# Hybrid SSD and attention block: shared inverse roots in the final norm, and the last halves weighted on the vector engine

## The chip, the cores and the metric

The kernel runs on one core of one Trainium2 chip. The metric is the device time of one execution in microseconds. Engines are named as in the profile: PE (TensorE matmul; PEld its weight loads), DVE (VectorE), ACT (ScalarE), POOL (GpSimd), SP (SyncE, which issues all transfers here).

## The reference

One layer of a hybrid decoder block on a 1024 x 1024 stream: a Mamba-2 branch and a windowed attention branch, mixed by gates, then a SwiGLU feed-forward part, then the final norm. The change lies in the last two lines: the down projection and the norm of its result.

```python
def rmsnorm(x, g):
    xf = x.astype(jnp.float32)
    y = xf * lax.rsqrt(jnp.mean(xf * xf, axis=-1, keepdims=True) + EPS)
    return (y * g.astype(jnp.float32)).astype(x.dtype)
...
        h = rmsnorm(x, norm_ffn[l])
        x = x + (jax.nn.silu(h @ w_ffn_gate[l]) * (h @ w_ffn_up[l])) @ w_ffn_down[l]
    return rmsnorm(x, norm_final)
```

## The kernel before

The stream x of 1024 tokens stands as eight row blocks of 128 tokens, numbered jj = 0 to 7; each block has two halves b = 0 and 1 of 512 columns. At the end of the kernel all of it lies in one tile xr (128 partitions, 8 blocks, 1024 columns), nfin holds norm_final on every partition, and jk takes the squares that nobody reads.

The down projection is done as seven matrix products after Strassen's and Winograd's scheme, in the order PRODUCTS = (1, 2, 3, 5, 7, 6, 4). The list INTO says to which quarters (th, b) of the output a product adds: th picks blocks 0 to 3 or 4 to 7, b the half. Each product has four row blocks j. Matrices are used as two parts, a high one (an ACT cast) and a low one (a DVE subtraction, "split" below), and every tile product takes three matmuls, so PE waits for these casts and splits. Products 6 and 4 are the last: product 6 adds to (0, 1), (1, 0) and (1, 1), which ends the work on blocks 0 to 3 and on the right halves of blocks 4 to 7; product 4 adds to (1, 0), the left halves of blocks 4 to 7. In product 4, the last four of the inner steps are run row block by row block (n_tail = 4), so block 4 is ended first and block 7 last.

down_out takes each result out of PSUM with a DVE SCALAR_TENSOR_TENSOR ("eviction" below: half of it is added to xr), and behind the final eviction of each half it starts out_half(jj, b). That function squares the half on ACT with a sum over the columns (tile osq, a slot of two sums for each block), multiplies the half by nfin on POOL in place, and, for the second half of a block, has inverse_root compute the root of that block's mean square by twelve 128x1 instructions on DVE: the sum, a shift and a subtraction on the bits for a first guess, and three Newton steps of three instructions each. Then ACT scales the right half, DVE the left half, and SP issues one transfer for each, 256 KB.

The order of instructions on each engine comes from a planner (the class Pace): it runs the kernel's tasks against estimated times, and a task issues its next instructions when the planner thinks that its inputs are there. For blocks 0 to 3 inverse_root yields to the planner behind every instruction, so that those roots are strewn between other work; for blocks 4 to 7 it does not, and a root stands in one piece. Small tiles come from the function small(tag, width), where each pair of tag and width has four slots in rotation. Every recorded instruction carries the line of the recording helper, L169, so rows are told apart by their tiles.

Of the kernel before, what the change touches and what calls it, by code (L numbers as in the profile page):

```python
# [14 lines left out]
AF = mybir.ActivationFunctionType  # L15
ALU = mybir.AluOpType
# [4 lines left out]
P = 128  # L21
S = 1024
D = 1024
# [9 lines left out]
EPS = 1e-6  # L33
# [303 lines left out]
def hybrid_block(ctx, tc, x, norm_mix, w_in, b_gate, conv_w, conv_b, dt_bias, a_log, d_skip, ssm_norm,  # L337
# [3 lines left out]
    nc = Core(tc.nc, pace)  # L341
    x, out = x[0], out[0]
# [22 lines left out]
    def nid():  # L365
        uid[0] += 1
        return uid[0]
# [84 lines left out]
    def small(tag, w):  # L452
        return kpool.tile([P, w], F32, tag=f"{tag}{w}", name=f"{tag}{w}_{nid()}", bufs=4)
# [38 lines left out]
    def plan_a(col):  # L492
        return [plan(cols_of(w_in, 0, KD, col, P), KD)]
# [853 lines left out]
    first = [plan_a(GATE0 + i * P)[0] for i in range(2)]  # L1347
# [723 lines left out]
    xr, nfin, jk = (lp.tile([P, n, D], F32, name=t) for t, n in (("xr", NCH), ("nfin", 1), ("jk", 1)))  # L2071
    nfin, jk = nfin[:, 0, :], jk[:, 0, :]
# [10 lines left out]

    sums = {}

    def inverse_root(v, r, t, sq):
        nc.vector.tensor_scalar(v, sq[:, 0:1], sq[:, 1:2], D * EPS, ALU.add, ALU.add)
        yield v
        nc.vector.tensor_scalar(t.bitcast(I32), v.bitcast(I32), 1, None, ALU.logical_shift_right)
        yield t  # L2090
        nc.vector.tensor_scalar(r.bitcast(I32), t.bitcast(I32), -1.0, 1597463007.0, ALU.mult, ALU.add)
        yield r
        for c in (1.0, 1.0, D ** 0.5):
            nc.vector.scalar_tensor_tensor(t, r, v, r, ALU.mult, ALU.mult)
            yield t
            nc.vector.tensor_scalar(t, t, -0.5 * c, 1.5 * c, ALU.mult, ALU.add)
            yield t
            nc.vector.tensor_tensor(r, r, t, ALU.mult)
            yield r

    def out_half(jj, b):
        first = jj not in sums
        if first:
            sums[jj] = small("osq", 2)
        xj = xr[:, jj, b * 512:(b + 1) * 512]
        yield [xr]
        nc.scalar.activation(jk[:, b * 512:(b + 1) * 512], xj, AF.Square, accum_out=sums[jj][:, b:b + 1])
        nc.gpsimd.tensor_tensor(xj, xj, nfin[:, b * 512:(b + 1) * 512], ALU.mult)
        if first:
            return  # L2110
        v, r, t = (small(n, 1) for n in ("ov", "or", "ot"))
        yield [sums[jj]]
        for w in inverse_root(v, r, t, sums[jj]):
            if jj < 4:
                yield [w]
        xj = xr[:, jj, :]
        rows = slice(jj * P, (jj + 1) * P)
        nc.scalar.activation(xj[:, 512:], xj[:, 512:], AF.Copy, scale=r)
        nc.vector.tensor_scalar(xj[:, :512], xj[:, :512], r, None, ALU.mult)
        nc.sync.dma_start(out[rows, :512], xj[:, :512])  # L2120
        nc.sync.dma_start(out[rows, 512:], xj[:, 512:])

    def down_out(p, ready, outs, done):
        for j in range(4):
            yield ready[j]
            for th, b in INTO[p]:
                yield 0.25 if p == PRODUCTS[-1] else 1.2
                xj = xr[:, th * 4 + j, b * 512:(b + 1) * 512]
                nc.vector.scalar_tensor_tensor(xj, outs[j], 0.5, xj, ALU.mult, ALU.add)
                if (p, th, b) in ((2, 0, 0), (6, 0, 1), (6, 1, 1), (4, 1, 0)):  # L2130
                    pace.spawn(out_half(th * 4 + j, b), 0.0, -1)
            done[j]()
# [59 lines left out]
```

## Time and profile before

| what | value |
|---|---|
| median of 3 runs | 2187.26 us (2186.94 to 2187.71) |
| the profiled execution, its own time | 2188.89 us |
| span of the profiled execution | 2187.1 us |
| granted TensorE clock, mean | 0.989 |
| PE busy, of the span | 2136.4 us, 98% |
| DVE busy | 1559.2 us, 71% |
| ACT busy | 903.6 us, 41% |
| POOL busy | 656.9 us, 30% |
| DMA issues of the output | 16 of 256 KB, 2.4 us to landing (median) |

The span runs from the first to the last instruction of the profiled execution; its own time holds 1.79 us more. A row of the timeline gives the start (us from the span's start), the duration, the engine, the line, the operation, out<-in, the shape and, in brackets, how long the engine sat idle before it and on what. A row of the windows gives the window, its length, then for PE, PEld, DVE, ACT and POOL the busy us with the number of instructions, then the granted clock, the busy share of the DMA engines and the GB/s moved.

### The profile page before, as it was taken

How to read it: one execution, taken by the hardware profiler on the slowest of the kernel's cores; microseconds unless marked ns; L12 is line 12 of the kernel's file. 1: busy time of each engine (PE TensorE's matmuls, PEld its weight loads, DVE VectorE, ACT ScalarE, POOL GpSimd, SP SyncE). 2: the span in 40 equal slices, each digit the busy share in tenths (PEclk: the TensorE clock that was granted, in tenths of full speed). 3: DMA queues.
4: the chain of work that ended last, by engine and by line, in shares of the span. 5: the costliest groups of instructions: out<-in, count | busy, mean ns of one | idle time of the engine just before them, and what ended most of it. 6: DMA issues, size and time to landing. Idle time of an engine off the chain costs nothing. (4 is left out here: it accounts for less than half of the span.)

```text
span 2187.1 us, 27856 instructions
## 1 busy us (share of the span) xinstructions
PE 2136.4 (98%) x10356; PEld 1764.4 (81%) x10356; DVE 1559.2 (71%) x2126; ACT 903.6 (41%) x1626; POOL 656.9 (30%) x426
## 2 busy tenths in 40 slices
PE   7999999999999999999999999999999999999996
PEld 6788878888887888788888887888778888888885
DVE  5687888867656787797754347544897777767787
ACT  4543444344355555455533224322333332324444
POOL 1233222332113454454431003011554544420002
PEclk8999999999999999999999999999999999999998
DMA  3533343434364566675486466354032323349332
GB/s 128 161 102 106 106 122 106 120 102 125 106 203 153 183 193 190 217 232 166 133 270 201 137 200 224 117 183 150 25 117 89 117 90 116 106 155 357 99 97 101
DMA packets 308939, 322.90 MB, mean 148 GB/s; under 512 B 20740, under 2 KB 246980, under 8 KB 308548
## 3 DMA queue, kind: packets, MB, share of 16 engines
q1 hardware_dynamic: 308804, 321.13, 46.3%
q8 instruction: 81, 1.33, 0.2%
q14 instruction: 54, 0.44, 0.1%
HBM read 236.54 MB, written 84.54 MB: 147 GB/s over the span
## 5 line engine op out<-in xcount | busy, mean ns | idle before, releaser
L169 POOL TENSOR_TENSOR xr<-xr,nfin 128x512 f32<-128x512 f32 x16 | 21.8, 1369 | 185.1 <-ACT jk L169 185.1
L169 POOL TENSOR_TENSOR slab__31_12297<-h2hi,h2lo 128x1024 f32<-128x1024 f32 x1 | 3.3, 3339 | 119.7 <-PE wide__54_11935 L169 119.7
L169 POOL TENSOR_TENSOR slab__29_10800<-slab__29_10800,last__1_10783 128x1024 f32<-128x1024 f32 x1 | 2.4, 2396 | 116.1 <-DMA slab__29_10800<-yt_d 116.1
L169 POOL TENSOR_TENSOR slab__3_5034<-slab__3_5034,slab__3_5032 128x1024 f32<-128x1024 f32 x1 | 2.4, 2396 | 69.2 <-DMA slab__3_5032<-in_rope 69.2
L169 POOL TENSOR_TENSOR slab__8_12293<-h2hi,h2lo 128x512 f32<-128x512 f32 x2 | 2.6, 1292 | 62.3 <-DVE h2lo L169 62.3
L169 ACT ACTIVATE jk<-xr 128x512 f32<-128x512 f32 x16 | 10.1, 632 | 15.4 <-DVE xr L169 11.2
L169 POOL TENSOR_TENSOR slab__2_644<-slab__2_642 128x512 f32<-128x512 f32 x1 | 4.0, 4017 | 37.6 <-DMA slab__2_642<-in_w_in 37.6
L169 PE MATMUL wide__1_208<-hhi,slab__1_272 128*128 128x256 f32 (+1 forms) x24 | 9.7, 403 | 2.2 <-ACT hhi L169 2.2
L169 PE MATMUL wide__1_208<-hlo,slab__1_272 128*128 128x256 f32 (+1 forms) x24 | 9.5, 397 | 2.1 <-DVE hlo L169 2.1
L169 POOL TENSOR_TENSOR slab__74_15692<-more__13_15384,slab__60_15505 128x512 f32<-128x512 f32 x1 | 1.3, 1297 | 32.1 <-DVE slab__60_15505 L169 32.1
L169 POOL TENSOR_TENSOR slab__1_620<-hhi,hlo 128x1024 f32<-128x1024 f32 x1 | 2.4, 2410 | 28.4 <-DVE hlo L169 28.4
L169 POOL TENSOR_TENSOR slab__14_10033<-slab__14_10033,slab__10_9841 128x1024 f32<-128x1024 f32 x1 | 2.5, 2505 | 26.2 <-DMA slab__14_10033<-yt_d 26.2
L169 ACT ACTIVATE xr<-xr,or 128x512 f32<-128x512 f32 x8 | 5.6, 717 | 11.3 <-DVE or L169 11.3
L169 DVE TENSOR_TENSOR hlo<-slab__1_624,hhi 128x1024 fp32r<-128x1024 f32 x1 | 1.2, 1225 | 11.8 <-ACT hhi L169 11.8
L169 DVE TENSOR_TENSOR slab__22_5025<-slab__19_4802,slab__19_5024 128x1024 fp32r<-128x1024 f32 x1 | 1.2, 1224 | 11.5 <-issue 11.5
L169 PE MATMUL wide__35_7344<-hhi,slab__25_7221 128*128 128x512 f32 x16 | 7.5, 466 | 1.7 <-DVE slab__6_7342 L169 1.7
L169 PEld LDWEIGHTS wide__1_208<-hlo,slab__1_272 128*128 128x128 f32 x24 | 5.8, 240 | 3.8 <-DVE hlo L169 3.6
L169 PE MATMUL wide__1_208<-hhi,slab__1_273 128*128 128x256 f32 (+1 forms) x24 | 8.8, 365 | 0.0
L169 PEld LDWEIGHTS wide__1_208<-hhi,slab__1_272 128*128 128x128 f32 x24 | 5.8, 240 | 3.6 <-ACT hhi L169 3.4
L169 PE MATMUL wide__30_5419<-hhi,slab__21_5293 128*128 128x512 f32 x16 | 8.0, 497 | 0.4 <-DVE slab__3_5413 L169 0.4
L169 PE MATMUL bank__1_210<-ident 128*128 128x128 f32 x36 | 5.7, 335 | 2.7 <-DMA ident<-in_consts 2.7
L169 POOL TENSOR_TENSOR slab__9_9508<-slab__9_9508,slab__4_9506 128x1024 f32<-128x1024 f32 x1 | 2.4, 2431 | 19.6 <-DMA slab__9_9508<-yt_d 19.6
(7946 smaller groups left out, 8299.5 us busy)
## 6 DMA issues: line engine op xcount, KB each, us to landing
xr<-x_d SPq DMA_DIRECT2D x8, 512.0 KB, 6.7
out<-xr SPq DMA_DIRECT2D x16, 256.0 KB, 2.4
b_d<-hhi SPq DMA_DIRECT2D x1, 1024.0 KB, 5.2
b_d<-hlo SPq DMA_DIRECT2D x1, 1024.0 KB, 7.3
slab__1_174<-in_x SPq DMA_DIRECT2D x1, 512.0 KB, 3.8
slab__1_175<-in_x SPq DMA_DIRECT2D x1, 512.0 KB, 5.0
slab__1_182<-in_norm_mix SPq DMA_DIRECT2D x1, 512.0 KB
slab__1_189<-in_w_in SPq DMA_DIRECT2D x1, 512.0 KB
```

Of the source, the lines that this page charges most:

```text
L169: r = call(*args, **kw)
```

## The change

Three things are changed in out_half and inverse_root. The row blocks form three groups, (0, 1, 2, 3), (4) and (5, 6, 7); a group has one tile of sums and one inverse root of the group's width, which is computed when the last half of the group has been squared, and behind it all blocks of the group are scaled and sent. The left halves of blocks 4 to 7 (b = 0, the last ones, flag late) are not multiplied by nfin on POOL; DVE's scaling of these halves becomes a SCALAR_TENSOR_TENSOR that multiplies by the root and by nfin. The root's arithmetic is another one, with the same three Newton steps: the mean square comes from the scale of the square, EPS is added in an instruction of its own, a factor −0.5 v is prepared, and there are 14 instructions in place of 12.

```diff
-    def inverse_root(v, r, t, sq):
-        nc.vector.tensor_scalar(v, sq[:, 0:1], sq[:, 1:2], D * EPS, ALU.add, ALU.add)
+    def inverse_root(v, r, t, h, sq):
+        nc.vector.tensor_tensor(v, sq[:, :, 0], sq[:, :, 1], ALU.add)
+        yield v
+        nc.vector.tensor_scalar(v, v, EPS, None, ALU.add)
         yield v
         nc.vector.tensor_scalar(t.bitcast(I32), v.bitcast(I32), 1, None, ALU.logical_shift_right)
+        nc.vector.tensor_scalar(h, v, -0.5, None, ALU.mult)
         yield t
         nc.vector.tensor_scalar(r.bitcast(I32), t.bitcast(I32), -1.0, 1597463007.0, ALU.mult, ALU.add)
         yield r
-        for c in (1.0, 1.0, D ** 0.5):
-            nc.vector.scalar_tensor_tensor(t, r, v, r, ALU.mult, ALU.mult)
+        for _ in range(3):
+            nc.vector.tensor_tensor(t, r, h, ALU.mult)
             yield t
-            nc.vector.tensor_scalar(t, t, -0.5 * c, 1.5 * c, ALU.mult, ALU.add)
+            nc.vector.tensor_tensor(t, t, r, ALU.mult)
             yield t
-            nc.vector.tensor_tensor(r, r, t, ALU.mult)
+            nc.vector.scalar_tensor_tensor(r, t, 1.5, r, ALU.add, ALU.mult)
             yield r
 
     def out_half(jj, b):
-        first = jj not in sums
-        if first:
-            sums[jj] = small("osq", 2)
+
+        group, n = ((0, 4), (4, 1), (5, 3))[(jj > 3) + (jj > 4)]
+        i = jj - group
+        if group not in sums:
+            sums[group] = [small("osq", 8)[:, :2 * n].rearrange("p (n b) -> p n b", b=2), 2 * n]
+        s = sums[group]
+        late = jj > 3 and b == 0
         xj = xr[:, jj, b * 512:(b + 1) * 512]
         yield [xr]
-        nc.scalar.activation(jk[:, b * 512:(b + 1) * 512], xj, AF.Square, accum_out=sums[jj][:, b:b + 1])
-        nc.gpsimd.tensor_tensor(xj, xj, nfin[:, b * 512:(b + 1) * 512], ALU.mult)
-        if first:
+        nc.scalar.activation(jk[:, b * 512:(b + 1) * 512], xj, AF.Square, scale=D ** -0.5, accum_out=s[0][:, i, b:b + 1])
+        if not late:
+            nc.gpsimd.tensor_tensor(xj, xj, nfin[:, b * 512:(b + 1) * 512], ALU.mult)
+        s[1] -= 1
+        if s[1]:
             return
-        v, r, t = (small(n, 1) for n in ("ov", "or", "ot"))
-        yield [sums[jj]]
-        for w in inverse_root(v, r, t, sums[jj]):
+        v, r, t, h = (small(k, 4)[:, :n] for k in ("rv", "rs", "rt", "sq"))
+        yield [s[0]]
+        for w in inverse_root(v, r, t, h, s[0]):
             if jj < 4:
                 yield [w]
...
+        for i in range(n):
+            rows = slice((group + i) * P, (group + i + 1) * P)
+            xj, ri = xr[:, group + i, :], r[:, i:i + 1]
+            nc.scalar.activation(xj[:, 512:], xj[:, 512:], AF.Copy, scale=ri)
+            if late:
+                nc.vector.scalar_tensor_tensor(xj[:, :512], xj[:, :512], ri, nfin[:, :512], ALU.mult, ALU.mult)
+            else:
+                nc.vector.tensor_scalar(xj[:, :512], xj[:, :512], ri, None, ALU.mult)
+            nc.sync.dma_start(out[rows, :512], xj[:, :512])
+            nc.sync.dma_start(out[rows, 512:], xj[:, 512:])
```

What this does to the order of instructions shows at three places; ahead of product 2's results the engines' orders are the same. A row reads: line, operation, out<-in, shape.

The first place is DVE in product 4, at the last splits (tiles as, more and slab are parts of the factors; ov, or and ot belong to a root). Before:

```order
L169 TENSOR_TENSOR as__15_17220<-slab__7_15826,as__15_17220 128x512
L169 SCALAR_TENSOR_TENSOR ot_45_17157<-or_44_17156,ov_43_17155 128x1
L169 TENSOR_TENSOR as__15_17237<-slab__43_17035,as__15_17237 128x512
L169 TENSOR_SCALAR ot_49_17198<-ov_47_17196 128x1
L169 TENSOR_TENSOR or_40_17121<-or_40_17121,ot_41_17122 128x1
L169 TENSOR_SCALAR ot_37_17077<-ot_37_17077 128x1
L169 TENSOR_TENSOR as__15_17241<-slab__7_15826,as__15_17241 128x512
L169 TENSOR_SCALAR ot_45_17157<-ot_45_17157 128x1
L169 TENSOR_TENSOR as__15_17247<-more__43_17079,as__15_17247 128x512
```

After (rv, rt, rs and sq belong to the root of blocks 0 to 3; wide is a PSUM tile of product 6):

```order
L169 TENSOR_TENSOR as__15_17164<-slab__7_15826,as__15_17164 128x512
L169 SCALAR_TENSOR_TENSOR xr<-wide__60_16853,xr 128x512
L169 TENSOR_TENSOR rv_34_17175<-osq_31_16158 128x4
L169 SCALAR_TENSOR_TENSOR xr<-wide__60_16853,xr 128x512
L169 TENSOR_TENSOR as__15_17183<-slab__43_17032,as__15_17183 128x512
L169 TENSOR_SCALAR rv_34_17175<-rv_34_17175 128x4
L169 TENSOR_SCALAR rt_36_17177<-rv_34_17175 128x4
L169 TENSOR_SCALAR sq_37_17178<-rv_34_17175 128x4
L169 TENSOR_SCALAR rs_35_17176<-rt_36_17177 128x4
L169 TENSOR_TENSOR as__15_17200<-slab__7_15826,as__15_17200 128x512
L169 TENSOR_TENSOR rt_36_17177<-rs_35_17176,sq_37_17178 128x4
L169 TENSOR_TENSOR as__15_17222<-more__43_17073,as__15_17222 128x512
```

The steps of four roots between the evictions of product 6 and the splits have become those of one root of width 4, which starts behind the last but one of these evictions; from the first output eviction of product 6 to the last split of product 4 there were 30 such small instructions, and are 8.

The second place is the end of DVE's queue, from the last eviction on (bank is a PSUM tile of product 4). Before:

```order
L169 SCALAR_TENSOR_TENSOR xr<-bank__175_17086,xr 128x512
L169 SCALAR_TENSOR_TENSOR xr<-bank__181_17087,xr 128x512
L169 TENSOR_SCALAR ot_49_17198<-ot_49_17198 128x1
L169 TENSOR_SCALAR xr<-xr,or_44_17156 128x512
L169 TENSOR_SCALAR ov_54_17354<-osq_42_17140 128x1
L169 TENSOR_SCALAR ot_56_17356<-ov_54_17354 128x1
```

After:

```order
L169 SCALAR_TENSOR_TENSOR xr<-xr,rs_39_17273,nfin 128x512
L169 SCALAR_TENSOR_TENSOR xr<-bank__173_17079,xr 128x512
L169 SCALAR_TENSOR_TENSOR xr<-bank__175_17080,xr 128x512
L169 SCALAR_TENSOR_TENSOR xr<-bank__181_17081,xr 128x512
L169 TENSOR_TENSOR rv_42_17350<-osq_33_17127 128x3
L169 TENSOR_SCALAR rv_42_17350<-rv_42_17350 128x3
```

Behind the last eviction stood a scaling and the roots and scalings of blocks 5, 6, 7 and, last, the scaling of block 3; now one root of width 3 and three weighted scalings stand there, and the scalings of blocks 0 to 3 and the whole of block 4 are ahead of the evictions of blocks 5 to 7.

The third place is ACT at the squares of product 6 (jk<-xr with its sum in osq), between the casts. Before:

```order
L169 ACTIVATE jk,osq_46_17178<-xr 128x512
L169 CAST as__15_17182<-slab__43_17035 128x512
L169 ACTIVATE jk,osq_34_16206<-xr 128x512
L169 ACTIVATE jk,osq_50_17216<-xr 128x512
L169 CAST as__15_17220<-slab__7_15826 128x512
L169 CAST as__15_17237<-slab__43_17035 128x512
```

After:

```order
L169 CAST as__15_17164<-slab__7_15826 128x512
L169 ACTIVATE jk,osq_31_16158<-xr 128x512
L169 CAST as__15_17183<-slab__43_17032 128x512
L169 ACTIVATE jk,osq_33_17127<-xr 128x512
L169 CAST as__15_17200<-slab__7_15826 128x512
```

Before, eight tiles osq share four slots, so osq_50 lies where osq_34 was; now there are three tiles, osq_31, 32 and 33, and a cast stands between the last two squares.

More of the change, by code (lines that the diff above doesn't have):

```diff
@@ L2114, in out_half @@
+        yield [s[0]]
+        for w in inverse_root(v, r, t, h, s[0]):
             if jj < 4:
                 yield [w]
[L2116 to L2121, printed above, removed]
+        for i in range(n):
[8 more added lines that the diff above has]
+            nc.sync.dma_start(out[rows, 512:], xj[:, 512:])
```

## The prediction

> **What bounds the kernel now.** I read the head of the page, then the busy time by stage, then the last 45 us of the timeline instruction by instruction, with what the engines wait for. The head gives the size; the table by stage (busy us and count of PE, PEld, DVE, ACT, POOL, then granted clock, DMA share, GB/s) says where the matmuls are over.
>
> ```profile
> span 2187.1 us, 27856 instructions
> ...
> 2175.00:2180.00 5.00, 0.00 (x0) 0.00 (x0) 4.13 (x22) 1.45 (x2) 0.00 (x0) 0.50 0.35 132
> 2180.00:2187.10 7.10, 0.00 (x0) 0.00 (x0) 1.95 (x8) 1.33 (x2) 0.00 (x0) 0.50 0.54 202
> ```
>
> From 2175 us on PE does nothing, and DVE is busy 4.13 us of 5 with 22 small instructions. The end is a tail behind the last matmul, and the change touches this tail and the 25 us ahead of it. In the timeline (start, us, engine) the tail reads:
>
> ```profile
> 2170.59 0.69 DVE L169 SCALAR_TENSOR_TENSOR xr<-bank__181_17087,xr 128x512 f32<-128x512 f32 x1 [1.18 <-PE bank__181_17087 L169]
> 2171.37 0.63 ACT L169 ACTIVATE jk<-xr 128x512 f32<-128x512 f32 x1 [1.11 <-DVE ot L169]
> 2171.91 0.18 ACT L169 ACTIVATION_READ_ACCUMULATOR jk<-xr 128x1 f32 x1
> ...
> 2178.28 0.48 DVE L169 TENSOR_SCALAR xr<-xr,or 128x512 f32<-128x512 f32 x1
> ...
> 2179.63 0.15 DVE L169 TENSOR_SCALAR ot<-ot 128x1 f32<-128x1 f32 x1
> 2179.81 0.16 DVE L169 TENSOR_TENSOR or<-or,ot 128x1 f32<-128x1 f32 x1
> ...
> 2180.01 0.22 DVE L169 SCALAR_TENSOR_TENSOR ot<-or,ov 128x1 f32<-128x1 f32 x1
> ...
> 2181.09 0.16 DVE L169 TENSOR_TENSOR or<-or,ot 128x1 f32<-128x1 f32 x1
> 2181.34 1.33 ACT L169 ACTIVATE xr<-xr,or 128x512 f32<-128x512 f32 x2 [2.35 <-DVE or L169]
> 2181.35 0.88 DVE L169 TENSOR_SCALAR xr<-xr,or 128x512 f32<-128x512 f32 x2
> 2181.87 1.80 SPq L169 DMA_DIRECT2D out<-xr  x4
> ```
>
> The last eviction (row block 7) waits for PE and starts at 2170.59. Its sum of squares is there at 2171.91 + 0.18 = 2172.09. But DVE first works through the roots of blocks 5 and 6, and reaches block 7's scaling only at 2181.35: the step from block 6's scaling to block 7's is 2181.35 − 2178.28 = 3.07 us, nearly all of it twelve dependent 128x1 instructions, which follow each other by 0.18 to 0.26. Then four output transfers (blocks 7 and 3) leave together:
>
> ```profile
> 2182.00:2183.00 1.00, 0.00 (x0) 0.00 (x0) 0.23 (x1) 0.68 (x2) 0.00 (x0) 0.50 0.29 109
> 2183.00:2184.00 1.00, 0.00 (x0) 0.00 (x0) 0.00 (x0) 0.00 (x0) 0.00 (x0) 0.50 1.04 389
> 2184.00:2185.00 1.00, 0.00 (x0) 0.00 (x0) 0.00 (x0) 0.00 (x0) 0.00 (x0) 0.50 1.01 375
> 2185.00:2186.00 1.00, 0.00 (x0) 0.00 (x0) 0.00 (x0) 0.00 (x0) 0.00 (x0) 0.50 0.47 176
> ```
>
> The four windows add up to 1.049 MB, which is 4 x 262,144 bytes. At a DMA share of 1 the rate is 389 and 375, mean 382 GB/s. So data begin about 109/389 = 0.28 us before 2183, at 2182.72 (0.85 after the first issue at 2181.87), end at 2185 + 176/382 = 2185.46, and the span ends 1.64 later.
>
> **The change part by part.** *One root for blocks 5 to 7.* New tail, counted from the start E of the last eviction. The square ends 2172.09 − 2170.59 = 1.50 later, and 0.03 passes to the first root instruction. The new root has 14 instructions, one (the factor −0.5) beside another, so 13 in a chain: twelve steps of 0.19 and a last one of 0.26 (2181.35 − 2181.09), 2.54 us. Width 3 in place of 1 I cost at nothing, since 0.15 us for one element is all fixed time; width 3 would have to triple it to matter. Two roots of block width are saved.
>
> *Weighting in the scaling.* Blocks 4 to 7 lose their POOL multiply of the last half, and DVE's scaling there becomes a SCALAR_TENSOR_TENSOR with three operands in SBUF. The same shape stands elsewhere in the trace, in two sizes:
>
> ```profile
> L169 DVE SCALAR_TENSOR_TENSOR slab__11_9861<-slab__9_9783,par,slab__13_9860 128x512 fp32r<-128x512 f32 x2 | 1.4, 738 | 0.0
> ...
> L169 DVE SCALAR_TENSOR_TENSOR slab__11_12894<-slab__11_12894,slab__31_12892 128x512 f32<-128x512 f32 x1 | 1.8, 1782 | 0.0
> ```
>
> I take 0.74, not 1.78: POOL has nothing left to do in the new tail, and the next rows show what POOL does to such instructions.
>
> ```profile
> 2172.17 1.27 POOL L169 TENSOR_TENSOR xr<-xr,nfin 128x512 f32<-128x512 f32 x1 [0.55 <-ACT jk L169]
> 2172.25 0.15 DVE L169 TENSOR_SCALAR or<-ot 128x1 int32<-128x1 int32 x1
> 2172.44 1.01 DVE L169 SCALAR_TENSOR_TENSOR ot<-or,ov 128x1 f32<-128x1 f32 x1
> ```
>
> While POOL multiplies, a one-tensor TENSOR_SCALAR takes its 0.15 us, but an instruction with several SBUF tensors sits until POOL's end at 2173.44 (1.01 where the same instruction took 0.22 at 2180.01). Leaving out the late multiplies takes this 0.8 us away too; it is contained in the new sum, which has no such stall.
>
> *The end.* First scaled half at E + 1.50 + 0.03 + 2.54 + 0.74 = E + 4.81, its transfer issued 0.04 later (as 2181.83 to 2181.87 before), data 0.85 after that: E + 5.70. Now six halves leave together, 1.573 MB at 382 GB/s, 4.12 us against 2.75 before; they are produced faster (a pair each 0.7 us is 750 GB/s) and issued faster (1.80/4 = 0.45 us each is 580 GB/s), so the rate decides. Data end at E + 9.82, span at E + 11.46. Saved time here goes partly into a longer burst: 1.4 us are given back.
>
> *Where E lies.* PE itself stalled before the tail, and DVE and ACT show why:
>
> ```profile
> 2152.98 0.20 DVE L169 TENSOR_SCALAR ov<-osq 128x1 f32<-128x1 f32 x1
> 2153.22 0.63 ACT L169 ACTIVATE jk<-xr 128x512 f32<-128x512 f32 x1 [2.21 <-DVE ov L169]
> 2154.48 1.38 DVE L169 TENSOR_TENSOR as__15_17220<-slab__7_15826,as__15_17220 128x512 fp32r<-128x512 f32 x1 [1.11 <-ACT as__15_17220 L169]
> 2155.75 0.90 PE L169 MATMUL bank__170_17084<-as__15_17220,as__15_17182 128*128 128x512 f32 x3
> 2160.90 0.68 DVE L169 TENSOR_TENSOR slab__57_17279<-slab__42_15909,slab__57_17279 128x512 fp32r<-128x512 f32 x1
> 2162.21 0.86 PE L169 MATMUL bank__173_17085<-as__15_17241,as__15_17237 128*128 128x512 f32 x3
> ...
> 2165.11 2.72 PE bank__175_17086 L169 x12
> ```
>
> Twelve matmuls take 2.72 us, so the eight groups of three from 2155.75 should end at 2161.19; the next group starts at 2162.21, 1.02 us late, held by DVE's last split (ended 2161.58). The split is late because ACT sat 2.21 us on a square whose accumulator slot (four of tag osq) was still to be read by block 3's first root step, the casts behind it came late, DVE waited 1.11, and because DVE carried the root steps of four blocks between its splits:
>
> ```profile
> L169 DVE SCALAR_TENSOR_TENSOR ot<-or,ov 128x1 f32<-128x1 f32 x7 | 2.0, 291 | 0.0
> L169 DVE TENSOR_SCALAR ot<-ot 128x1 f32<-128x1 f32 x6 | 0.8, 139 | 0.0
> L169 DVE TENSOR_SCALAR ov<-osq 128x1 f32<-128x1 f32 x4 | 0.8, 202 | 0.2 <-ACT jk L169 0.2
> L169 DVE TENSOR_TENSOR or<-or,ot 128x1 f32<-128x1 f32 x5 | 0.7, 145 | 0.0
> L169 DVE TENSOR_SCALAR or<-ot 128x1 int32<-128x1 int32 x4 | 0.6, 141 | 0.0
> L169 DVE TENSOR_SCALAR ot<-ov 128x1 int32<-128x1 int32 x4 | 0.6, 138 | 0.0
> ...
> 2150.12 0.13 DVE L169 TENSOR_SCALAR ot<-ot 128x1 f32<-128x1 f32 x1
> 2150.18 0.13 DVE L169 TENSOR_SCALAR ot<-ov 128x1 int32<-128x1 int32 x1
> ```
>
> These are the 128x1 groups between 2139.5 and 2161.6: 30 instructions. The order after the change has eight of 128x4 there, and three accumulator tiles where four slots exist, so no square waits for a slot. 22 fewer at 0.06 each (2150.12 to 2150.18) are 1.3 us, and the 1.11 of waiting may go. Against this stands one new block: the shared root now begins with a TENSOR_TENSOR, which POOL can hold up to its 1.3 us, with an eviction and eight splits queued behind it on DVE. Net, the last split should end about 1.1 us earlier (1.3 + 1.11 − 1.3), so PE's stall goes whole; bounds 0 and 1.02 (a later E than before is excluded while the block costs less than the two gains together). I take 1.02: E = 2169.57.
>
> The Trainium skill ("SBUF — State Buffer", section "SBUF: two separate sides") speaks against this change: the port pair of DVE and GpSimd is an exclusive lock for a whole instruction, and a DVE instruction with two SBUF inputs takes part in it against a GpSimd instruction that reads SBUF. By that rule the first step of the shared root queues behind POOL, where the TENSOR_SCALAR of before did not; the rows at 2172 agree (1.01 against 0.15). With it deciding, E stays at 2170.59, the first rival below; without it, E is as I take it.
>
> *What DVE must do by then.* Behind the last split: six root steps (1.14), block 4's eviction 0.69, four scalings, block 4's root 2.54, its weighted scaling 0.74, two evictions 1.38.
>
> ```profile
> L169 DVE TENSOR_SCALAR xr<-xr,or 128x512 f32<-128x512 f32 x8 | 4.0, 504 | 0.4
> ```
>
> With 4 x 0.50 this is 8.5 us, from about 2160.3 to 2168.8, 0.8 ahead of E; the evictions of 5 and 6 now queue behind block 4's root, but PE needs no bank back, so nobody waits. ACT's four scalings stand ahead of block 4's and end in time (1.33 for two above). The eight transfers of blocks 0 to 3 now all leave near 2163 to 2166, need 5.5 us at 382 GB/s, and are gone by 2171.
>
> **Sum.** Span 2169.57 + 11.46 = 2181.03 against 2187.1: 6.07 us less (1.02 PE, 5.05 tail). The profiled execution took 2188.89 (1.79 around the span), so 2182.8; the median of the runs is 2187.26, so **2181.2**. 0.2% is 4.4 us, about what a measurement here can tell from no change.
>
> **The rivals.**
> - *PE's stall stays.* The POOL block on the shared root eats what DVE gains. For it: the rows at 2172. Against it: 22 instructions and an ACT wait go. 2182.2. Chance 0.18.
> - *The weighted scalings take 1.78 us.* The first half is then not 0.74 but 1.78, and the third ends 2173.64 + 5.34 = 2178.98; issue 0.04, second half's issue 0.45, 0.85 and one transfer of 0.69, then 1.64: span 2182.65, time 2182.8. The rows of 1.78 stand against those of 0.74, and POOL's silence is for 0.74. Alone 0.05; with the stall kept too 2183.8, which is within 0.2%: 0.07.
> - *The change does not do what it says,* the roots being hidden behind transfers: 2187.3. Against it: DVE is busy 4.13 of 5 us with no transfer between most roots. 0.04.
> - *Slower: the burst of six.* Blocks 5 and 6 used to leave alone, each behind its own root; now three blocks wait for block 7 and share the 16 DMA engines at the very end. It costs more than is saved if 1.573 MB need over 4.12 + 6.07 us, below 154 GB/s. The page's row of rates ends with 101 for the slice of the tail:
>
> ```profile
> GB/s 128 161 102 106 106 122 106 120 102 125 106 203 153 183 193 190 217 232 166 133 270 201 137 200 224 117 183 150 25 117 89 117 90 116 106 155 357 99 97 101
> ```
>
> At 101 GB/s the burst takes 15.6 us: 2181.2 + 15.6 − 4.1 = 2192.7. But that average holds idle time; at full share the rate was 375 to 389. 0.03.
>
> **How the numbers follow.** Forecast 0.63, and the rivals as given. Low end: root steps of 0.155 (their own duration) save 0.5, and the runs scatter by 0.4: 2180.3. High end: stall kept and slow scalings, 2183.8. Faster: 0.63 + 0.18 + half of the 0.05 that lies at the bound, 0.84; same 0.07 + 0.04 + 0.02, 0.13; slower 0.03.
>
> **What would show it.** In the new profile: the last eviction at 2169.6 (2170.6: stall kept); no ACT wait for DVE of 2 us near 2153; 14 root rows of 128x3 in about 2.5 us; three weighted scalings of 0.74; one burst of six transfers of some 4.1 us near 380 GB/s; span 2181.0. A late last eviction that waits for DVE and not for PE, or a burst well under 380 GB/s, would make it wrong.

## The result, and the profile after

| | before | after |
|---|---|---|
| median, runs side by side | 2187.87 us (2186.94 to 2188.88, 6 runs) | 2204.48 us (2199.74 to 2204.76, 6 runs) |
| profiled execution, its span | 2187.1 us | 2202.4 us |
| start E of the last eviction | 2170.59 us | 2191.06 us |
| from E to the end of the span | 16.51 us | 11.34 us |

The ratio after to before is 1.0075 (95% interval 1.0064 to 1.0087): 16.6 us slower, where 2181.2 was forecast. The last row says that the tail did what the prediction says of it; the row above it says that the program arrives there 20.47 us late. So the loss lies ahead of the tail. The head of the page after:

```profile
span 2202.4 us, 27795 instructions
...
PE 2157.2 (98%) x10356; PEld 1764.7 (80%) x10356; DVE 1553.8 (71%) x2072; ACT 902.9 (41%) x1626; POOL 653.2 (30%) x422
```

PE is busy 98% as before, but for 20.8 us more (2136.4 before). In stages where PE hardly stops, the table by stage counts how many matmuls it got through. Before:

```profile
100.00:500.00 400.00, 398.16 (x1789) 329.20 (x1788) 325.88 (x414) 168.71 (x267) 121.69 (x84) 1.00 0.37 112
...
1600.00:2000.00 400.00, 398.65 (x1758) 329.56 (x1757) 292.74 (x383) 128.16 (x220) 160.99 (x110) 1.00 0.40 133
2000.00:2140.00 140.00, 140.00 (x619) 115.91 (x618) 113.79 (x166) 61.90 (x113) 6.28 (x5) 1.00 0.44 139
```

After:

```profile
100.00:500.00 400.00, 397.80 (x1761) 323.88 (x1760) 326.98 (x413) 166.15 (x263) 120.50 (x83) 1.00 0.36 109
...
1600.00:2000.00 400.00, 397.30 (x1721) 322.80 (x1722) 293.67 (x376) 124.40 (x211) 167.48 (x114) 1.00 0.36 117
2000.00:2140.00 140.00, 140.00 (x619) 115.84 (x618) 112.11 (x164) 62.52 (x114) 6.07 (x4) 1.00 0.54 181
```

At a granted clock of 1.00 in both, 1789 matmuls became 1761 and 1758 became 1721, though PE's instructions there are the same in the same order. In the last stage 619 stayed 619. So neither the clock nor the DMA load is the cause (DMA is lower in the two slow stages and higher in the equal one), and not all matmuls are slower. Two runs of twelve matmuls show which; first the same twelve before:

```profile
1750.28 0.39 PE L169 MATMUL bank__158_14080<-h2hi,slab__20_13835 128*128 128x512 f32 x1
...
1753.00 0.39 PE L169 MATMUL bank__148_14097<-slab__53_12654,slab__19_13847 128*128 128x512 f32 x1
```

and after, with twelve others of the same kernel, from 1317.73 to 1320.45:

```profile
1317.73 0.39 PE L169 MATMUL wide__49_10782<-slab__12_9903,slab__46_10794 128*128 128x512 f32 x1
...
1320.45 0.39 PE L169 MATMUL wide__49_10782<-slab__8_10079,slab__46_10794 128*128 128x512 f32 x1
...
1767.86 0.40 PE L169 MATMUL bank__158_14080<-h2hi,slab__20_13835 128*128 128x512 f32 x1
...
1770.66 0.39 PE L169 MATMUL bank__148_14097<-slab__53_12654,slab__19_13847 128*128 128x512 f32 x1
```

Twelve matmuls on h2hi or h2lo and a slab took 2.72 us before and take 2.80 after: 0.2267 and 0.2333 us each. Twelve on two slabs take 2.72 after too. The program places its tiles in SBUF from both ends of each partition's addresses: slab and more lie on the left side, the low addresses, and h2hi, h2lo, hhi, hlo, xr and as on the right side, the high ones; what became slower are matmuls with one operand on each side.

The starts of the same matmul in both timelines, after minus before (medians over stretches of 25 us), show it as a drift that grows and rests:

| us of before | 25 | 250 | 625 | 900 | 1225 | 1300 | 1350 | 1450 | 1650 | 1950 | 2025 |
|---|---|---|---|---|---|---|---|---|---|---|---|
| after − before, us | −1.1 | 2.3 | 7.1 | 6.0 | 9.4 | 9.4 | 13.2 | 13.2 | 16.0 | 21.1 | 21.2 |

It rests in some stretches, as where both operands are slabs (1225 to 1300, the rows above) and from 1950 on, and grows in all the others but for single steps. All but 0.2 us of the drift had come by 1950, and up to 2139 us of before the instructions of PE, DVE, ACT and POOL are the same in the same order. The largest step, some 3 us near 1325, is of another kind: PE waits there in both kernels for one split on DVE (slab__34), which stands behind two scalings and another split. Before:

```profile
1321.95 3.56 DVE L169 SCALAR_TENSOR_TENSOR slab__14_10887<-slab__29_10812,par,slab__11_10886 128x512 fp32r<-128x512 f32 x2
...
1329.46 0.50 PE L169 MATMUL bank__136_10900<-slab__34_10952,h2hi 128*128 128x512 f32 x1 [3.26 <-DVE slab__34_10952 L169]
...
1330.00:1340.00 10.00, 10.00 (x38) 8.08 (x37) 9.04 (x9) 3.40 (x6) 1.67 (x1) 0.83 0.20 63
```

and after:

```profile
1331.47 5.69 DVE L169 SCALAR_TENSOR_TENSOR slab__14_10887<-slab__29_10812,par,slab__11_10886 128x512 fp32r<-128x512 f32 x2
...
1341.14 0.79 PE L169 MATMUL bank__136_10900<-slab__34_10952,h2hi 128*128 128x512 f32 x1 [5.29 <-DVE slab__34_10952 L169]
...
1340.00:1350.00 10.00, 8.86 (x28) 7.02 (x29) 7.23 (x8) 3.23 (x4) 0.00 (x0) 0.68 0.01 2
```

PE's wait is 2.0 us longer (5.29 against 3.26) because the two scalings took 5.69 us in place of 3.56, and the clock granted behind the wait is lower (0.68 against 0.83).

How much is the pace and how much are the waits shows when the time from each matmul's start to the next is compared, matmul by matmul, and the differences are added up by kind:

| behind which matmuls | how many | after − before, us | each, us |
|---|---|---|---|
| 128x512, one operand on each side | 4418 | 22.7 | 0.0051 |
| 128x512, both on one side | 3504 | 1.0 | 0.0003 |
| other shapes | 2103 | 0.4 | 0.0002 |
| steps above 0.3 us in either kernel (waits, low clock) | 330 | −3.5 | |

Together that is 20.5 us. The pace of the first kind makes more than the whole loss; the waits, the step near 1325 included, give 3.5 us back.

The tail after, by the timeline:

```profile
2177.15 0.85 PE L169 MATMUL bank__170_17078<-as__15_17164,as__15_17143 128*128 128x512 f32 x3
...
2182.62 0.86 PE L169 MATMUL bank__173_17079<-as__15_17200,as__15_17183 128*128 128x512 f32 x3
...
2191.06 0.69 DVE L169 SCALAR_TENSOR_TENSOR xr<-bank__181_17081,xr 128x512 f32<-128x512 f32 x1 [1.56 <-PE bank__181_17081 L169]
...
2192.59 0.16 DVE L169 TENSOR_TENSOR rv<-osq 128x3 f32<-128x3 f32 x1 [0.85 <-ACT jk L169]
2192.79 0.17 DVE L169 TENSOR_SCALAR rv<-rv 128x3 f32<-128x3 f32 x1
...
2195.16 2.08 DVE L169 SCALAR_TENSOR_TENSOR xr<-xr,rs,nfin 128x512 f32<-128x512 f32 x3
```

and its windows:

```profile
2196.00:2197.00 1.00, 0.00 (x0) 0.00 (x0) 1.00 (x2) 1.00 (x2) 0.00 (x0) 0.68 0.22 82
2197.00:2198.00 1.00, 0.00 (x0) 0.00 (x0) 0.24 (x1) 0.11 (x1) 0.00 (x0) 0.50 1.04 387
2198.00:2199.00 1.00, 0.00 (x0) 0.00 (x0) 0.00 (x0) 0.00 (x0) 0.00 (x0) 0.50 1.02 371
2199.00:2200.00 1.00, 0.00 (x0) 0.00 (x0) 0.00 (x0) 0.00 (x0) 0.00 (x0) 0.50 1.03 387
2200.00:2201.00 1.00, 0.00 (x0) 0.00 (x0) 0.00 (x0) 0.00 (x0) 0.00 (x0) 0.50 0.93 346
```

The eight groups of product 4 take 2182.62 − 2177.15 = 5.47 us, 0.03 over their 5.44. The root takes 2195.16 − 2192.59 = 2.57, and the five windows add up to the 1.573 MB of six halves.

### The profile page after: what moved, and what is told of

Its sections match the earlier page's. It is cut to its first block, busy times and chain, and to the rows that moved or that the text cites. A ratio compares the mean times of both kernels' runs of the same rounds, so it can differ in the third digit from the quotient of the medians.

```text
span 2202.4 us, 27795 instructions
## 1 busy us (share of the span) xinstructions
PE 2157.2 (98%) x10356; PEld 1764.7 (80%) x10356; DVE 1553.8 (71%) x2072; ACT 902.9 (41%) x1626; POOL 653.2 (30%) x422
## 5 line engine op out<-in xcount | busy, mean ns | idle before, releaser
L169 POOL TENSOR_TENSOR xr<-xr,nfin 128x512 f32<-128x512 f32 x12 | 17.3, 1451 | 172.6 <-ACT jk L169 172.2
L169 PEld LDWEIGHTS bank__1_210<-ident 128*128 128x128 f32 x36 | 6.7, 208 | 2.7 <-DMA ident<-in_consts 2.7
L169 DVE SCALAR_TENSOR_TENSOR slab__36_10850<-slab__29_10800,par,slab__35_10849 128x512 fp32r<-128x512 f32 x2 | 5.4, 2746 | 4.8 <-ACT slab__35_10849 L169 4.8
L169 PE MATMUL wide__35_7344<-hhi,slab__25_7221 128*128 128x512 f32 x16 | 6.9, 432 | 1.8 <-DVE slab__6_7342 L169 1.8
```

The source lines that it names most:

```text
L169: r = call(*args, **kw)
```

## The experiments

**The theory: the change moved the left side of SBUF.** Small tiles come from one pool at the bottom of SBUF, with four slots of 32 bytes for each pair of tag and width. The tags osq of width 2 and ov, or and ot of width 1 go, 16 slots of 32 bytes, 512 bytes; osq of width 8 comes, 4 slots, 128 bytes. rv, rs, rt and sq of width 4 were there already for other work. By this count the pool is 384 bytes shorter, and all that lies above it on the left side starts 384 bytes lower: the first slab at byte 6400 of each partition in place of 6784. The right side is placed from the top and stays (hhi at 163712). Counted in steps of 256 bytes, slabs and hhi stood alike before (both 128 over a multiple); after the change they stand 128 apart ("distance" below: data start minus weight start, what is left over a multiple of 256). Two constants, K_PAD and R_PAD (line 49), set the widths in float32 words of two unused tiles ahead of the left and the right side, so that each side can be shifted without touching an instruction.

The rival is that something in the program itself (the new order, the burst, another engine) makes PE slower. It predicts that a shift changes nothing.

**Experiment 1: the change, with the left side put back to 6784.**

```diff
-K_PAD, R_PAD = 40, 24
+K_PAD, R_PAD = 136, 24
```

> The changed kernel with the small pool's pad made 96 floats longer (K_PAD 136 for 40), which puts every buffer of the left side of SBUF back to the addresses of the kernel before (first slab at byte 6784, 128 modulo 512; 6400 and 256 in the changed kernel). Nothing else differs. Theory 'placement' (the change shortens the small pool by 384 bytes, and TensorE's matmuls become slower by where their operands lie): every 128x512 matmul is back at a mean of 389 ns, and what is left is the gain that was predicted: 2181 us, 2180 to 2184. Rival 'the change's own work' (something in the new instructions slows the whole program): stays at 2200 to 2205 us.

**Experiment 2: the kernel before, with its left side moved by 128 bytes** (6912, a distance of 128 as after the change).

```diff
-K_PAD, R_PAD = 40, 24
+K_PAD, R_PAD = 72, 24
```

> The kernel before with the small pool's pad made 32 floats longer (K_PAD 72 for 40): the left side starts at byte 6912, 256 modulo 512, as in the changed kernel, and the distance to the right side (hhi, h2hi, xr at 384 modulo 512) is 128 modulo 512 as there. No instruction differs. Theory 'placement': the slow matmuls of the changed kernel (395 ns for 389 where one operand lies left and the other right) appear here too, and the kernel before becomes slower by about 20 us: 2205 to 2210 us. Rival 'the change's own work': no effect, 2187 to 2189 us.

**Experiment 3: the change, with the right side moved down by 384 bytes instead** (slabs at 6400, hhi at 163328).

```diff
-K_PAD, R_PAD = 40, 24
+K_PAD, R_PAD = 40, 120
```

> The changed kernel with the pad of the right side made 96 floats longer (R_PAD 120 for 24): the left side stays at 256 modulo 512, the right side moves from 384 to 0 modulo 512, so that their distance is 256 modulo 512 again, as in the kernel before, at other addresses. If the distance of the two operands decides: 2180 to 2184 us, 389 ns. If the address of the left side alone decides: stays at 2200 to 2205 us.

**Experiment 4: the change, with the left side at 6528,** 128 over a multiple of 256 as hhi, but at another multiple than before.

```diff
-K_PAD, R_PAD = 40, 24
+K_PAD, R_PAD = 72, 24
```

> The changed kernel with K_PAD 72: left side at 384 modulo 512, the same as the right side, distance 0 modulo 512. Two operands of one side have distance 0 and run at 389 ns in both kernels; if the distance decides and 0 is as good as 256, 2180 to 2184 us. If only the distance 256 is good, or the left address of 128 modulo 512: 2195 us or more.

Measured, each beside the kernel before (its median in these runs 2186.81 us):

| | distance mod 256 | median, us | ratio to before (95%) | from E to the end |
|---|---|---|---|---|
| 1: change, left back | 0 | 2178.93 | 0.9959 (0.9945 to 0.9973) | 11.41 |
| 2: before, left moved | 128 | 2209.93 | 1.0099 (1.0084 to 1.0114) | 16.55 |
| 3: change, right moved | 0 | 2183.93 | 0.9984 (0.9975 to 0.9993) | 11.18 |
| 4: change, left elsewhere | 0 | 2179.42 | 0.9958 (0.9943 to 0.9973) | 11.43 |

The first stage of experiment 1, where the change by itself had 1761 matmuls:

```profile
100.00:500.00 400.00, 397.66 (x1796) 328.69 (x1795) 323.82 (x414) 170.27 (x269) 122.06 (x85) 1.00 0.37 113
```

and of experiment 2, where the kernel before had 1789:

```profile
100.00:500.00 400.00, 397.79 (x1764) 323.91 (x1763) 325.68 (x413) 165.51 (x263) 118.02 (x82) 1.00 0.36 110
```

An unused tile turns the loss off in the change and on in the kernel before, so the rival falls: neither order nor arithmetic is needed for it. Experiments 1 and 4 came out 1.1 and 0.6 us below the 2180 to 2184 that was expected, 2 and 3 within their ranges. The starts of the matmuls in experiment 2 run away from those of before in the same stretches as in the table above. Experiments 3 and 4 say that no side and no one address is at fault but the distance: either side may be moved.

The four leave a difference: 3 ends some 5 us above 1 and 4, at the same distance. Comparing the starts of the same matmuls, 3 falls behind 1 by 1.3 us in the first 50 us, 0.8 near 275 and 2.8 near 1325 and is about level between. In the first of these places the granted clocks differ (before, then experiment 1):

```profile
0.00:50.00 50.00, 34.42 (x205) 31.09 (x206) 29.98 (x61) 22.49 (x36) 9.60 (x8) 0.83 0.43 140
```

```profile
0.00:50.00 50.00, 34.61 (x210) 31.03 (x211) 30.53 (x61) 23.37 (x38) 9.59 (x8) 0.90 0.42 140
```

3 has 0.83 there, as before has, and from 275 to 285 us 0.83 where experiment 1 has 1.00. Near 1325 both have 0.83 behind the wait, and what differs is the wait, 2.64 us in experiment 1 and 5.47 in 3. Experiment 1's split slab__34, then POOL and the same split in experiment 3:

```profile
1324.23 1.21 DVE L169 TENSOR_TENSOR slab__34_10952<-slab__38_10837,slab__46_10951 128x1024 fp32r<-128x1024 f32 x1
```

```profile
1327.06 2.38 POOL L169 TENSOR_TENSOR more__2_11028<-more__2_11028,last__2_11026 128x1024 f32<-128x1024 f32 x1 [0.36 <-DMA more__2_11028<-yt_d]
1327.17 3.36 DVE L169 TENSOR_TENSOR slab__34_10952<-slab__38_10837,slab__46_10951 128x1024 fp32r<-128x1024 f32 x1
```

In 3 a POOL multiply starts 0.11 us ahead of the split, and the split ends 1.09 behind POOL's end, so it sat until then. These few us thus come at places where PE waits, from the clock granted there or from POOL's hold on DVE, and not from the matmuls' pace. Whether the shift of the right side brings that about or chance does was not tried.

**Experiment 5: TensorE alone.** A kernel of its own, which computes nothing of the block: groups of 48 matmuls of the shape above (each with its own 128x128 weight load) from two tiles, wt and mv, behind a group for warming up. It ran once. The starts of the weights (groups w), of the data (m) or of both (s) are shifted by 0, 32, ... 480 bytes, letters a to p.

```diff
+            for i in range(16):
+                o = group("w" + letters(i), i % 8, i * STEP, 0, REPS)
+            for i in range(16):
+                o = group("m" + letters(i), i % 8, 0, i * STEP, REPS)
+            for i in range(16):
+                o = group("s" + letters(i), i % 8, i * STEP, i * STEP, REPS)
```

> A kernel of its own that computes nothing of the reference: 48 groups of 48 matmuls (128x128 weights, 128x512 moving data, fp32r, as in the kernel), each with a new weight load, one after the other with nothing else running. In groups wa to wp the weights start 0, 32, 64 ... 480 bytes past a multiple of 512 bytes from the moving data; in ma to mp the moving data are shifted instead; in sa to sp both are shifted together (distance 0). If the distance alone decides and TensorE alone is enough to show it: 0.227 us for each matmul at distances 0 and 256, about 0.233 at 128 and 384 (wa, wi, ma, mi fast, we, wm, me, mm slow), and all of sa to sp at 0.227. If it takes other engines' traffic on SBUF: 0.227 everywhere. If the address of one operand alone decides: sa to sp differ as well.

From its timeline (a group's time is the start of the next group less its own):

```profile
107.76 11.32 PE L44 MATMUL we<-mv,wt 128*128 128x512 f32 x48
118.91 11.37 PE L44 MATMUL wf<-mv,wt 128*128 128x512 f32 x48
130.12 11.16 PE L44 MATMUL wg<-mv,wt 128*128 128x512 f32 x48
141.12 11.36 PE L44 MATMUL wh<-mv,wt 128*128 128x512 f32 x48
152.31 11.05 PE L44 MATMUL wi<-mv,wt 128*128 128x512 f32 x48
163.20 11.35 PE L44 MATMUL wj<-mv,wt 128*128 128x512 f32 x48
...
241.38 11.04 PE L44 MATMUL ma<-mv,wt 128*128 128x512 f32 x48
252.25 11.37 PE L44 MATMUL mb<-mv,wt 128*128 128x512 f32 x48
```

| group | data minus weights, mod 256 | 48 matmuls | one |
|---|---|---|---|
| ma (nothing shifted) | 0 | 10.87 | 0.2265 |
| wi (weights by 256) | 0 | 10.89 | 0.2269 |
| wg (weights by 192) | 64 | 11.00 | 0.2292 |
| we (weights by 128) | 128 | 11.15 | 0.2323 |
| wf, wh (by 160, 224) | 96, 32 | 11.21, 11.19 | 0.2335, 0.2331 |
| mc, me (data by 64, 128) | 64, 128 | 11.00, 11.20 | 0.2292, 0.2333 |
| wd, mf (weights by 96, data by 160) | 160, 160 | 11.24, 11.24 | 0.2342, 0.2342 |

wa, the first group and unshifted as ma, takes 11.00, because of one step of 0.33 us at its start; its last forty matmuls go at 0.2267. With both shifted together the groups sa to so take 10.89 to 10.92 (sp has no group behind it). So TensorE by itself shows it, with no other engine at work: only the distance of weights and data counts (groups of one distance agree within 0.05 us, wa apart), with a period of 256 bytes, and it is worth up to 0.008 us in 0.227. The two paces of the kernel, 0.2267 and 0.2333, are those of distance 0 and of a distance off 0. Which part of the chip makes this distance matter no run tells.

**Experiments 6 to 8: the parts of the change and the accumulator slots,** each with the left side placed at a distance of 0.

Experiment 6, the shared roots alone; POOL multiplies the last halves as before:

```diff
-K_PAD, R_PAD = 40, 24
+K_PAD, R_PAD = 136, 24
...
-        late = jj > 3 and b == 0
+        late = False
```

> The changed kernel at the placement of the kernel before (K_PAD 136), with the grouped roots alone: all halves are still weighted by POOL, and DVE scales with the one-tensor form. If the grouped roots carry the tail's gain: a ratio of about 0.996 against the kernel before as with both parts, the span ending about 11.6 us behind the last eviction (16.5 in the kernel before; 11.4 with both). If the weighting carries it: no more than 1 us faster than the kernel before, 0.9995.

Experiment 7, the weighting alone, in the kernel before, with a root for each block:

```diff
-        nc.gpsimd.tensor_tensor(xj, xj, nfin[:, b * 512:(b + 1) * 512], ALU.mult)
+        late = jj > 3 and b == 0
+        if not late:
+            nc.gpsimd.tensor_tensor(xj, xj, nfin[:, b * 512:(b + 1) * 512], ALU.mult)
...
-        nc.vector.tensor_scalar(xj[:, :512], xj[:, :512], r, None, ALU.mult)
+        if late:
+            nc.vector.scalar_tensor_tensor(xj[:, :512], xj[:, :512], r, nfin[:, :512], ALU.mult, ALU.mult)
+        else:
+            nc.vector.tensor_scalar(xj[:, :512], xj[:, :512], r, None, ALU.mult)
```

> The kernel before (placement unchanged) with the other part alone: the last halves of blocks 4 to 7 are weighted by DVE in the scaling, each block keeps its own root. If the grouped roots carry the gain: within 0.2% of the kernel before, the span ending 16 to 16.5 us behind the last eviction (POOL's hold of 0.8 us on a root step goes, three scalings get 0.27 longer). If the weighting carries it: 0.996.

Experiment 8, the kernel before with eight accumulator slots in place of four:

```diff
-K_PAD, R_PAD = 40, 24
+K_PAD, R_PAD = 8, 24
...
-            sums[jj] = small("osq", 2)
+            sums[jj] = kpool.tile([P, 2], F32, tag="osq2", name=f"osq2_{nid()}", bufs=8)
```

> The kernel before with eight slots for the sums of squares in place of four, the pad of the small pool shortened by as much (K_PAD 8), so that placement and the order of instructions are as before. If the wait for a slot is what made ACT late (2.21 us) and with it DVE's last split: that wait is gone, the last split ends about 1 us earlier and most of PE's 1.02 us stall goes; time 0.5 to 1 us lower at most, which is within 0.2%. If DVE's root steps between the splits make it late: the stall stays at 0.7 us or more.

| | median, us | before, us | ratio (95%) | from E to the end | PE's stall in product 4 |
|---|---|---|---|---|---|
| 6: shared roots alone | 2182.03 | 2186.17 | 0.9975 (0.9966 to 0.9985) | 12.78 | 0 |
| 7: weighting alone | 2184.51 | 2186.17 | 0.9989 (0.9980 to 0.9997) | 14.92 | 1.00 |
| 8: eight slots | 2187.1 | 2186.17 | 1.0001 (0.9992 to 1.0010) | 16.45 | 0.22 |

Experiment 6 ends its tail 1.37 us later than experiment 1. Its timeline shows why:

```profile
2166.46 3.71 POOL L169 TENSOR_TENSOR xr<-xr,nfin 128x512 f32<-128x512 f32 x3 [4.75 <-ACT jk L169]
2166.72 0.69 DVE L169 SCALAR_TENSOR_TENSOR xr<-bank__181_17081,xr 128x512 f32<-128x512 f32 x1 [0.56 <-PE bank__181_17081 L169]
...
2168.26 0.71 DVE L169 TENSOR_TENSOR rv<-osq 128x3 f32<-128x3 f32 x1 [0.85 <-ACT jk L169]
2169.01 1.19 DVE L169 TENSOR_SCALAR rv<-rv 128x3 f32<-128x3 f32 x1
```

POOL works through three multiplies until 2170.17, and the root's first two instructions, which take 0.16 and 0.17 in the tail after, take 0.71 and 1.19; the second ends with POOL at 2170.20. That is 1.57 us, of which the shorter scaling without nfin gives 0.2 back. So the weighting in the scaling is worth 1.4 us of the tail, by silencing POOL while the shared root runs. Neither side of the expectation came, 11.6 us of tail if the shared roots carry all and next to no gain if the weighting does: the roots by themselves carry 3.7 of the 5.1 us.

Experiment 7 gains 1.59 us of the tail, where 0 to 0.5 was expected (16 to 16.5 us from E to the end) if the roots carry the gain. From its timeline:

```profile
2166.38 0.69 DVE L169 SCALAR_TENSOR_TENSOR xr<-bank__181_17087,xr 128x512 f32<-128x512 f32 x1 [1.46 <-PE bank__181_17087 L169]
...
2176.78 0.75 DVE L169 SCALAR_TENSOR_TENSOR xr<-xr,or,nfin 128x512 f32<-128x512 f32 x1
```

and its last windows with data:

```profile
2178.00:2179.00 1.00, 0.00 (x0) 0.00 (x0) 0.00 (x0) 0.00 (x0) 0.00 (x0) 0.50 0.62 233
2179.00:2180.00 1.00, 0.00 (x0) 0.00 (x0) 0.00 (x0) 0.00 (x0) 0.00 (x0) 0.50 0.78 291
```

The three roots still follow each other, with the last weighted scaling at E + 10.40 against E + 10.76 before. The rest comes from the burst: 0.524 MB are left at the end, two halves and not four, since block 3's halves now leave earlier.

Experiment 8 shows what PE's stall hung on. Its rows, to be read like the 2155.75 and 2162.21 of before:

```profile
2154.91 0.84 PE L169 MATMUL bank__170_17084<-as__15_17220,as__15_17182 128*128 128x512 f32 x3
...
2160.57 0.86 PE L169 MATMUL bank__173_17085<-as__15_17241,as__15_17237 128*128 128x512 f32 x3
```

5.66 us in place of 6.46: the slots alone take 0.8 of the 1.02 us away, with all thirty small root instructions still between the splits. The median doesn't tell 8 from before, as 0.8 us is within its interval.

## Why the prediction was wrong

- **The step that failed is "Where E lies".** It took E = 2170.59 − 1.02 = 2169.57, that is: all ahead of product 2's results costs what it cost, because the orders there are the same. The orders are the same; the addresses are not. E came at 2191.06, and by the sum above the slower pace of the matmuls with one operand on each side cost 22.7 us. Neither the forecast nor any rival, the slower one included, had a cost of matmuls in it. With the addresses alone put right (experiment 1), the time is 2178.93, ratio 0.9959 (0.9945 to 0.9973), where the forecast's 2181.2 to 2187.26 is 0.9972. Its E, 2165.39, lies 5.2 us ahead of before's; the stall gives 1.0 of that, and 4.2 had come by 1400 us, at places where PE had idled. Experiment 7, whose instructions are those of before up to 2163 us, is ahead by the same 4.2 us there, so they are no part of the change. Of the 10.3 us between the spans of before and experiment 1, 6.1 are the forecast's (1.0 and 5.1) and 4.2 are luck of these executions.
- **PE's stall goes whole.** Right: 1.02 us became 0.03 (0.01 in experiment 1). As to its two causes, experiment 8 gives 0.8 us to the slot, and with the slots free 0.2 is left for the 22 instructions, for which the prediction added 1.3 us; what they would bring by themselves, with four slots, no run shows. The listed sign, no ACT wait of 2 us for DVE, was a poor one: in experiment 1 ACT still waits 2.37 us at 2149.85, now for an eviction of xr, and PE doesn't feel it.
- **POOL's hold on the shared root.** The row of experiment 1:

```profile
2148.21 0.65 DVE L169 TENSOR_TENSOR rv<-osq 128x4 f32<-128x4 f32 x1
...
2151.56 0.84 PE L169 MATMUL bank__170_17078<-as__15_17164,as__15_17143 128*128 128x512 f32 x3
...
2157.01 0.86 PE L169 MATMUL bank__173_17079<-as__15_17200,as__15_17183 128*128 128x512 f32 x3
```

  The Trainium skill ("SBUF — State Buffer", section "SBUF: two separate sides") has a DVE instruction with two SBUF inputs and a GpSimd instruction that reads SBUF exclude each other for whole instructions, and the 0.65 beside a POOL multiply that ends at 2148.84, in place of 0.16 in the tail, agrees. It was sized at up to 1.3 us and cost 0.5. The first rival, in which this keeps the stall, did not come: 5.45 us pass, 0.01 over the 5.44 without a stall.
- **The tail.** Right in each term. Root 2.57 (2.54 said); the three weighted scalings 2.08 in all (3 x 0.74 said, against a rival of 3 x 1.78); data begin at 2197 − 82/382 = 2196.79, E + 5.73 (5.70 said), and end at 2200 + 346/382 = 2200.91, E + 9.85 (9.82 said). The six transfers ran at 371 to 387 GB/s, so the slower rival, a burst below 154 GB/s, fell. From E to the end 11.34, 11.41, 11.18 and 11.43 us in the four kernels with the change, against 11.46. The last eviction waited for PE (1.56 us) and not for DVE, as said; the 2160.3 in that count should be 2160.5 by its own 1.1 us, and nothing hangs on it.
- **The weighting's price.** It was costed at 0.74 us in place of 0.48 for the scaling, and as removing 0.8 us of held instructions. Experiment 6 puts it at 1.4 us, because with the shared root two instructions are held in a row, one of them a one-tensor TENSOR_SCALAR, which the prediction took to be safe from POOL by a 128x1 row.

So the local sum of 6 us stood, and the whole was wrong by 23, because a change of small tiles was taken to have no effect where no instruction changes. Experiments 1 and 4, the change with one constant set anew, beat both kernels.

## What to carry to other kernels

A tile that grows, shrinks or goes shifts every tile that is placed behind it, and the price of that can be larger than that of the edit: compare the start addresses of the big operands before and after a change, and if the time moves where no instruction did, put the addresses back with padding before looking for another cause. Where matmuls of this kind (128x128 fp32 weights, loaded anew for each 128x512 of data) make up the time, place the weights and the data a multiple of 256 bytes apart; other types and widths were not tried alone. And where a few small instructions set the end, look whether POOL is at work beside them.

## What was not expected of the hardware

- A 128x512 matmul with its own weight load takes 0.227 us where weights and data start at a distance of 0 mod 256 bytes, 0.229 at 64 (data minus weights), and 0.232 to 0.234 at the other distances tried (experiment 5). The same instructions took 2178.93 us with the two sides at a distance of 0 and 2204.48 at 128 (experiment 1 and the change).
- A 128x3 TENSOR_SCALAR with one tensor in SBUF was held by POOL for 1.19 us (experiment 6), where one of 128x1 passed in 0.15 beside a POOL multiply before the change.
- One wait of PE can differ by 2.8 us between kernels with the same instructions: near 1325 us PE waits in all of these kernels for the same split on DVE, for 2.64 us in experiment 1 and 5.47 in experiment 3, where POOL holds the split for 3.36 us in place of 1.21. Behind the wait the granted clock falls as well, to 0.83 before and to 0.68 after.
